# Sixteen 64-byte reads of the weights at the head of ScalarE's DMA queue, in a bilinear kernel

## Chip, core and metric

The kernel runs on one core of one Trainium2 chip. The metric is the device time of one execution in microseconds; where several executions were made, their median is given.

## What is computed

```python
batch, dim_i, dim_j, dim_k = 32, 256, 256, 128
# x [32, 256], y [32, 256], weight [128, 256, 256], all float32
out = np.einsum('bi,bj,kij->bk', x, y, weight)      # [32, 128] float32
```

For each k the 256 x 256 matrix of weights is multiplied from the left by a row of x and from the right by a row of y. The weights are 33.55 MB and are read once.

## The kernel before

**Layout.** The 128 values of k are cut into 32 groups of 4 (`G = 32`, `KK = 4`). A group is a tile of 128 partitions (4 values of k by 32 blocks of i) with 8 x 256 elements each (`IC = 8` rows of i by 256 of j), 1 MB in float32. TensorE multiplies the tile by a block-diagonal copy of x (`xblk`, 128 x 128 in bfloat16 for each of the 8 `ic`), adds the 8 steps up in PSUM, and gets for each k and batch row a row of 256 values of j. VectorE multiplies this by y (`y4`) and sums over j into `acc`, one column per group. At the end `acc` goes to the output in one DMA.

**Loads.** Thirty of the 32 groups are loaded by GpSimd's DMA queue (line 120, eleven transfers, listed in `LOADS`), which casts float32 to bfloat16 on the way into `w_sb`. The sizes fall towards the end: 2, 4, 8, 8, 4, 2 and 1 groups, then the last group in four parts. The other two groups (`FIRST`, 0 and 16) are loaded as float32 by SyncE's queue (line 133) into `w_f`, and ScalarE casts them into `w_sb` (line 177, four instructions). x and y are loaded by ScalarE's queue (lines 128 and 129). Each transfer has a semaphore of its own, waited for at 16.

**Order.** All these DMA instructions are moved by hand to the head of the program (`head[:at_hw] + hw + head[at_hw:at_sw] + sw + head[at_sw:]`), ahead of a start barrier that releases all engines at about 5.5 us. So ScalarE's queue begins with x and y, SyncE's with the two float32 groups, GpSimd's with its eleven loads. Behind the barrier ScalarE does its table load and its casts; VectorE makes `x_rep` (line 191), `xt` (197), `mask` (204), `xblk` (209) and then, from y, `yt` (218), `y_rep` (221) and `y4` (226).

**Compute.** `UNITS` gives the order in which groups are used: 16, 8, 4, 2, 1 and 1 groups. TensorE runs one unit after the other (matmul at line 236), each waiting for the loads that it needs and for free PSUM banks; VectorE follows with a product (293) and a sum (297), or both in one instruction for the two last units (301). Line 310 stores the output, and line 314 clears the semaphores, while SyncE waits for the store.

Of the kernel before, what the change touches and what calls it, by code (L numbers as in the profile page):

```python
# [36 lines left out]
def kernel(  # L37
# [7 lines left out]
    nc = tc.nc  # L45
    P = 128
    f32 = mybir.dt.float32
# [18 lines left out]
    def sbuf(name, shape, dtype):  # L66
        return nc.alloc_sbuf_tensor(name, shape, dtype).ap()

    def rows_of(groups):


        step = G // len(groups)
        assert all(g == groups[0] + n * step for n, g in enumerate(groups))
        v = weight.rearrange("(u s) (ip ic) j -> s ip u (ic j)", s=step, ic=IC)
        return v[groups[0]]

    def w_of(groups):
        at = [place_of[g] for g in groups]
        step = at[1] - at[0] if len(at) > 1 else 1
        assert all(a == at[0] + n * step for n, a in enumerate(at))  # L80
        return w_sb[:, at[0]:at[-1] + 1:step, :]

    w_sb = sbuf("w_sb", [P, G, IC * J], bf16)
    w_f = sbuf("w_f", [P, len(FIRST), IC * J], f32)
    x_sb = sbuf("x_sb", [B, I], f32)
    y_sb = sbuf("y_sb", [B, J], f32)
    ident = sbuf("ident", [P, P], f32)
# [12 lines left out]
    s_w = [nc.alloc_semaphore(f"w{n}") for n in range(len(LOADS))]  # L100
    sem_of = {
        (g, ic): s
        for s, (groups, lo, hi) in zip(s_w, LOADS) for g in groups for ic in range(lo, hi)
    }
    s_f = [nc.alloc_semaphore(f"f{g}") for g in FIRST]
    s_x = nc.alloc_semaphore("x")
    s_y = nc.alloc_semaphore("y")
    s_pool = nc.alloc_semaphore("pool")
    s_act = nc.alloc_semaphore("act")
    s_pe = nc.alloc_semaphore("pe")  # L110
    s_dve = nc.alloc_semaphore("dve")
    s_fin = nc.alloc_semaphore("fin")
    s_out = nc.alloc_semaphore("out")
    sems = [*s_w, *s_f, s_x, s_y, s_pool, s_act, s_pe, s_dve, s_fin]
    nums = [s.num for s in sems]
    assert nums == list(range(nums[0], nums[0] + len(nums)))

# [3 lines left out]
            out=w_of(groups)[:, :, lo * J:hi * J],  # L121
            in_=rows_of(groups)[:, :, lo * J:hi * J],
        ).then_inc(s, 16).ins
        for (groups, lo, hi), s in zip(LOADS, s_w)
    ]

    hw = [
        nc.scalar.dma_start(out=x_sb, in_=x).then_inc(s_x, 16).ins,
        nc.scalar.dma_start(out=y_sb, in_=y).then_inc(s_y, 16).ins,
    ]  # L130
    for n, g in enumerate(FIRST):
        hw.append(
            nc.sync.dma_start(
                out=w_f[:, n:n + 1, :], in_=rows_of((g,)),
# [13 lines left out]
    for blk in blocks:  # L148
# [15 lines left out]
    pool, act, v, pe, sp = nc.gpsimd, nc.scalar, nc.vector, nc.tensor, nc.sync  # L164
# [4 lines left out]
        out=ident, in_=ident, compare_op=mybir.AluOpType.not_equal, fill=1.0,  # L169
        base=0, pattern=[[-1, P]], channel_multiplier=1,  # L170
    )._wait_ge(s_pool, 1).then_inc(s_pool, 1)


    for n, g in enumerate(FIRST):
        for h in range(2):
            lo, hi = h * IC * J // 2, (h + 1) * IC * J // 2
            c = act.copy(out=w_sb[:, place_of[g], lo:hi], in_=w_f[:, n, lo:hi])  # L177
            if h == 0:
                c._wait_ge(s_f[n], 16)
            c.then_inc(s_act, 1)  # L180
# [4 lines left out]
    def done(ins):  # L185
# [6 lines left out]
        out=x_rep,  # L192
        in_=x_sb.rearrange("b (ip ic) -> b ic ip", ic=IC).unsqueeze(3)
        .to_broadcast([B, IC, IP, KK]),
    )._wait_ge(s_x, 16))
    for q in range(Q):
        c = v.transpose(  # L197
            out=xt[q * 32:(q + 1) * 32, :, :],
            in_=x_rep[:, :, q * IP // Q:(q + 1) * IP // Q, :],
# [5 lines left out]
        out=mask, in_=ident.rearrange("p (ip kk) -> p kk ip", kk=KK), axis=AX, op=add,  # L205
    )._wait_ge(s_pool, 2))

    for kk in range(KK):
        c = v.tensor_scalar(  # L209
            out=xblk[:, :, :, kk], in0=xt, scalar1=mask[:, kk:kk + 1],  # L210
# [8 lines left out]
        out=yt, in_=y_sb.rearrange("b (jb j) -> b jb j", j=32),  # L219
    )._wait_ge(s_y, 16))  # L220
    t = done(v.tensor_copy(  # L221
        out=y_rep, in_=yt.unsqueeze(3).to_broadcast([B, J // 32, B, KK]),
    )._wait_ge(s_dve, t))
    BQ = B // Q
    for q in range(Q):
        c = v.transpose(  # L226
            out=y4[q * 32:(q + 1) * 32, :].rearrange("p (jb j) -> p jb j", j=32),
            in_=y_rep[:, :, q * BQ:(q + 1) * BQ, :],
# [22 lines left out]
    for u, unit in enumerate(UNITS):  # L251
# [40 lines left out]
        if n_g > 1:  # L292
            t = done(v.tensor_tensor(  # L293
                out=prod, in0=sums, in1=y4.unsqueeze(1).to_broadcast([P, n_g, J]), op=mult,
# [3 lines left out]
                out=acc[:, unit[0]:unit[-1] + 1:unit[1] - unit[0]], in_=prod, axis=AX, op=add,  # L298
            )._wait_ge(s_dve, t))
        else:  # L300
            done(v.tensor_tensor_reduce(  # L301
                out=prod[:, 0, :], in0=sums[:, 0, :], in1=y4, scale=1.0, scalar=0.0,
# [44 lines left out]
```

## Time and profile before

| | |
|---|---|
| median of 9 runs | 84.71 us (84.62 to 84.98) |
| the profiled execution | 84.66 us, its span 83.4 us (83.36) |
| granted TensorE clock, mean | 0.959 |
| busy in the span | PE 33.8 us, DVE 24.7, ACT 5.3, POOL 8.3 |
| read from HBM | 33.62 MB |

The span runs from the first to the last instruction of the program; the execution's own time has 1.3 us more around it. Times in the profile count from the start of the span. The DMA queues are named by number: q0 is GpSimd's, q1 SyncE's, q10 ScalarE's. All of them run on the same 16 DMA engines of the core. The bytes of a packet are those written: a 4096-byte packet of q0 has read 8192 bytes of float32. The trace keeps the start, size, duration and queue of every packet, not the engine that moved it; a packet of 4 bytes is the write that counts a semaphore up.

### The profile page before, as it was taken

The numbers are of one execution on the slowest core, as the hardware profiler recorded it, in microseconds if no ns is written. First come the engines' busy times: TensorE is split into PE (matmuls) and PEld (weight loads), VectorE is DVE, ScalarE is ACT, GpSimd is POOL, SyncE is SP. The second block draws the span as 40 slices with busy tenths as digits, with TensorE's granted clock in tenths as the row PEclk, the third lists the DMA queues.
The fourth block names the chain that finished last, engine by engine and source line by source line (L and its number), as shares of the span: only waits on it lengthen the run. The fifth ranks groups of instructions, "written<-read, shape, count | busy, mean of one in ns | idle before, by whom it ended". The sixth has DMA issues, their size and how long they took to land.

```text
span 83.4 us, 257 instructions
## 1 busy us (share of the span) xinstructions
PE 33.8 (41%) x136; PEld 4.3 (5%) x43; DVE 24.7 (30%) x28; ACT 5.3 (6%) x5; POOL 8.3 (10%) x17
## 2 busy tenths in 40 slices
PE   0000000000000000000099999999007999999780
PEld 0000000000000000000000000000000000122330
DVE  0038596000000000000000000000999930299992
ACT  0039920000000000000000000000000000000000
POOL 5999300000000000000000000000000000000000
PEclk9999999999999999999999999999965579999999
DMA  3999999999999999999999999999999999999970
GB/s 134 379 383 291 218 210 220 216 212 210 212 218 218 218 210 212 212 218 220 214 210 214 212 218 218 218 210 212 212 218 218 216 210 214 210 220 216 195 112 8
DMA packets 4928, 17.91 MB, mean 215 GB/s; under 512 B 384, under 2 KB 832, under 8 KB 4672
## 3 DMA queue, kind: packets, MB, share of 16 engines
q0 software_dynamic: 4400, 15.73, 94.2%
q1 hardware_dynamic: 432, 2.11, 6.5%
q10 hardware_dynamic: 96, 0.07, 0.3%
HBM read 33.62 MB, written 0.02 MB: 404 GB/s over the span
## 4 chain that ended last, share of the span: by engine, by line
DMA 47%; PE 41%; DVE 6%; POOL 2%; issue 1%; another core or an unknown queue 1%; POOLq 0%
DMA w_sb<-in_weight_dram 47%; PE ps L236 41%; DVE tmp L293 5%; POOL w_sb L120 2%; DVE tmp L301 1%; POOL const-float32-0.0 L331 0%; POOLq L331 0%; POOL const-uint8-127 L331 0%; POOL const-float32-1.0 L331 0%; DVE acc L301 0%
## 5 line engine op out<-in xcount | busy, mean ns | idle before, releaser
L236 PE MATMUL ps<-w_sb,xblk 128*128 128x512 bf16 (+1 forms) x136 | 33.8, 410 | 47.6 <-DMA w_sb<-in_weight_dram 42.9
L293 DVE TENSOR_TENSOR tmp<-ps,y 128x4096 f32<-128x4096 f32 (+3 forms) x4 | 8.6, 2153 | 49.8 <-PE ps L236 49.8
L297 DVE TENSOR_REDUCE acc<-tmp 128x16 f32<-128x4096 f32 (+3 forms) x4 | 8.6, 2154 | 0.1
L236 PEld LDWEIGHTS ps<-w_sb,xblk 128*128 128x128 bf16 x43 | 4.3, 101 | 76.9 <-DMA w_sb<-in_weight_dram 42.7
L120 POOL DMA_DIRECT2D w_sb<-in_weight_dram x11 | 7.5, 699 | 0.6 <-issue 0.6
L177 ACT CAST w_sb<-w_f 128x1024 bf16<-128x1024 f32 x4 | 4.0, 1042 | 0.1
L191 DVE COPY x_rep<-x_sb 32x1024 f32<-32x1024 f32 x1 | 0.7, 736 | 5.6 <-PEq L331 5.6
L226 DVE STREAM_TRANSPOSE y<-y_rep 32x256 f32<-32x256 f32 x4 | 1.7, 434 | 0.1
L197 DVE STREAM_TRANSPOSE xt<-x_rep 32x256 f32<-32x256 f32 x4 | 1.7, 434 | 0.1
L177 ACT ACT_TABLE_LOAD x1 | 1.3, 1283 | 5.6 <-PEq L331 5.6
L209 DVE TENSOR_SCALAR xblk<-xt,mask 128x256 bf16<-128x256 f32 x4 | 1.4, 501 | 0.0
L301 DVE CUSTOM_DVE_ANT_0 tmp<-ps,y 128x256 f32<-128x256 f32 x2 | 0.8, 420 | 0.3 <-PE ps L236 0.3
L221 DVE COPY y_rep<-yt 32x1024 f32<-32x1024 f32 x1 | 0.7, 680 | 0.0
L204 DVE TENSOR_REDUCE mask<-ident 128x4 f32<-128x128 f32 x1 | 0.4, 383 | 1.0 <-POOL ident L168 1.0
L218 DVE STREAM_TRANSPOSE yt<-y_sb 32x256 f32<-32x256 f32 x1 | 0.4, 449 | 0.0
L168 POOL TENSOR_SCALAR_AFFINE_SELECT ident<-ident 128x128 f32<-128x128 f32 x1 | 0.3, 290 | 0.1
L167 POOL MEMSET ident<- 128x128 f32 x1 | 0.3, 279 | 0.0
L301 DVE DVE_READ_ACCUMULATOR2_ANT acc<- 128x1 f32 x2 | 0.2, 84 | 0.0
L331 POOL MEMSET const-float32-0.0<- 128x1 f32 x1 | 0.1, 99 | 0.2 <-issue 0.2
L331 POOL MEMSET const-bfloat16-1.0<- 128x1 bf16 x1 | 0.1, 102 | 0.0
L331 POOL MEMSET const-uint8-127<- 128x1 uint8 x1 | 0.1, 102 | 0.0
L331 POOL MEMSET const-float32-1.0<- 128x1 f32 x1 | 0.1, 99 | 0.0
## 6 DMA issues: line engine op xcount, KB each, us to landing
w_sb<-in_weight_dram POOLq DMA_DIRECT2D x2, 4096.0 KB, 48.5
w_sb<-in_weight_dram POOLq DMA_DIRECT2D x2, 2048.0 KB, 43.6
w_f<-in_weight_dram SPq DMA_DIRECT2D x2, 1024.0 KB, 6.8
w_sb<-in_weight_dram POOLq DMA_DIRECT2D x2, 1024.0 KB, 41.2
w_sb<-in_weight_dram POOLq DMA_DIRECT2D x1, 512.0 KB, 72.6
w_sb<-in_weight_dram POOLq DMA_DIRECT2D x1, 256.0 KB, 73.3
w_sb<-in_weight_dram POOLq DMA_DIRECT2D x1, 128.0 KB, 73.4
w_sb<-in_weight_dram POOLq DMA_DIRECT2D x2, 64.0 KB, 73.1
```

The lines of the kernel that those rows point to most:

```text
L120: nc.gpsimd.dma_start(out=w_of(groups)[:, :, lo * J:hi * J], in_=rows_of(groups)[:, :, lo * J:hi * J],).then_inc(s, 16).ins
L177: c = act.copy(out=w_sb[:, place_of[g], lo:hi], in_=w_f[:, n, lo:hi])
L191: t = done(v.tensor_copy(out=x_rep, in_=x_sb.rearrange("b (ip ic) -> b ic ip", ic=IC).unsqueeze(3) .to_broadcast([B, IC, IP, KK]),)._wait_ ...
L197: c = v.transpose(out=xt[q * 32:(q + 1) * 32, :, :], in_=x_rep[:, :, q * IP // Q:(q + 1) * IP // Q, :],)
L204: t = done(v.tensor_reduce(out=mask, in_=ident.rearrange("p (ip kk) -> p kk ip", kk=KK), axis=AX, op=add,)._wait_ge(s_pool, 2))
L209: c = v.tensor_scalar(out=xblk[:, :, :, kk], in0=xt, scalar1=mask[:, kk:kk + 1], scalar2=None, op0=mult,)
L221: t = done(v.tensor_copy(out=y_rep, in_=yt.unsqueeze(3).to_broadcast([B, J // 32, B, KK]),)._wait_ge(s_dve, t))
L226: c = v.transpose(out=y4[q * 32:(q + 1) * 32, :].rearrange("p (jb j) -> p jb j", j=32), in_=y_rep[:, :, q * BQ:(q + 1) * BQ, :],)
L236: return pe.add_instruction(mybir.InstMatmult(name=nc.get_next_instruction_name(), engine=mybir.EngineType.PE, ins=[pe.lower_ap(rhs), pe.l ...
L293: t = done(v.tensor_tensor(out=prod, in0=sums, in1=y4.unsqueeze(1).to_broadcast([P, n_g, J]), op=mult,)._wait_ge(s_pe, n_pe))
L297: done(v.tensor_reduce(out=acc[:, unit[0]:unit[-1] + 1:unit[1] - unit[0]], in_=prod, axis=AX, op=add,)._wait_ge(s_dve, t))
L301: done(v.tensor_tensor_reduce(out=prod[:, 0, :], in0=sums[:, 0, :], in1=y4, scale=1.0, scalar=0.0, op0=mult, op1=add, accum_out=acc[:, uni ...
```

## The change

ScalarE's queue gets a first transfer, ahead of x and y: 16 rows of 16 float32 values (64 bytes) from the first matrix of the weights, 16 KB apart, one row to each of 16 partitions of a new small tile `touch`. Nothing reads the tile. ScalarE waits for its semaphore ahead of its casts, and the semaphore joins those that are cleared at the end.

```diff
+    touch = sbuf("touch", [16, 16], f32)
...
+    s_touch = nc.alloc_semaphore("touch")
...
-    sems = [*s_w, *s_f, s_x, s_y, s_pool, s_act, s_pe, s_dve, s_fin]
+    sems = [*s_w, *s_f, s_touch, s_x, s_y, s_pool, s_act, s_pe, s_dve, s_fin]
...
     hw = [
+        nc.scalar.dma_start(
+            out=touch, in_=weight[0].rearrange("(e r) j -> e (r j)", e=16)[:, :16],
+        ).then_inc(s_touch, 16).ins,
         nc.scalar.dma_start(out=x_sb, in_=x).then_inc(s_x, 16).ins,
         nc.scalar.dma_start(out=y_sb, in_=y).then_inc(s_y, 16).ins,
     ]
...
+    act.wait_ge(s_touch, 16)
     for n, g in enumerate(FIRST):
```

In the order of the instructions on each engine, ScalarE's queue has one DMA more at its head and its table load one wait more. The order on the other four engines is as before.

## The prediction

> **What bounds the kernel now.** I read the table of queues first, then the chain that ended last, then the waits of TensorE, then the first 5 us in half-microsecond stretches, because the change acts only there.
>
> ```profile
> q0 software_dynamic: 4400, 15.73, 94.2%
> q1 hardware_dynamic: 432, 2.11, 6.5%
> q10 hardware_dynamic: 96, 0.07, 0.3%
> HBM read 33.62 MB, written 0.02 MB: 404 GB/s over the span
> ```
>
> GpSimd's queue (q0) and SyncE's (q1) hold the 16 DMA engines for about the whole span. The weights are 33.55 MB in float32, so nearly all that is read is the weights. In the packet records each engine takes one 8 KB piece every 305 ns (8 groups, 64 pieces per engine, land 19.52 us apart). 256 pieces per engine by 0.305 us is 78.1 us of the 83.4 us. The kernel is its stream of weights, and what is left is when the stream starts, what is put between its packets, and 2.6 us behind its last byte.
>
> ```profile
> 75.88 0.14 another core or an unknown queue
> ...
> 77.95 0.53 another core or an unknown queue
> ...
> 79.55 0.18 another core or an unknown queue
> ```
>
> These lines of the chain of waits, between pieces of TensorE work, are late landings of weights: TensorE has caught up by 75.9 us. If the stream ended earlier by up to 0.5 us, TensorE would follow. The last matmul, the product on VectorE and the output store come behind that and don't change.
>
> ```profile
> 1.00:1.50 0.50, 0.00 (x0) 0.00 (x0) 0.00 (x0) 0.00 (x0) 0.44 (x1) 1.00 0.49 174
> 1.50:2.00 0.50, 0.00 (x0) 0.00 (x0) 0.00 (x0) 0.00 (x0) 0.50 (x2) 1.00 0.71 285
> 2.00:2.50 0.50, 0.00 (x0) 0.00 (x0) 0.00 (x0) 0.00 (x0) 0.50 (x1) 1.00 1.07 442
> ...
> 3.50:4.00 0.50, 0.00 (x0) 0.00 (x0) 0.00 (x0) 0.00 (x0) 0.50 (x2) 1.00 1.09 369
> 4.00:4.50 0.50, 0.00 (x0) 0.00 (x0) 0.00 (x0) 0.00 (x0) 0.50 (x2) 1.00 0.86 324
> 4.50:5.00 0.50, 0.00 (x0) 0.00 (x0) 0.00 (x0) 0.00 (x0) 0.50 (x1) 1.00 1.01 410
> ```
>
> The last column is GB/s. Two dips matter: the stream isn't at full rate before 2.0 us, and it loses some between 3.5 and 4.5 us, which is where y's small packets come through. At full rate (16 engines by 8192 bytes per 305 ns: 430 GB/s) the second dip is 0.5 x (1 - 369/430) + 0.5 x (1 - 324/430) = 0.19 us.
>
> The first dip has a shape. In the packet records x (two packets of 1 KB and a semaphore write on each engine) starts at 1.18 us; on 13 engines its semaphore is written by 1.42 us. The first weight packets start at 1.41 to 1.66 us on twelve engines, about 0.15 us behind that engine's x semaphore. On three engines x's second packet comes at 1.78 to 1.90 us, and four engines start on the weights only at 1.96 to 2.07 us. The table of queues for 1.45 to 3.40 us shows the late ones:
>
> ```profile
> q1 hardware_dynamic: 88, 0.72, 91.7%
> q10 hardware_dynamic: 6, 0.00, 0.5%
> ```
>
> Six packets on ScalarE's queue: three late x packets and three semaphore writes. The lag never heals, for all engines run at one rate. The sixteen landings of the first GpSimd load spread from 11.64 to 12.23 us, those of the fourth load over 0.60 us too, the last ones from 80.26 to 80.77 us. TensorE needs all sixteen. So the end is set by an engine some 0.5 us behind the earliest, and its four followers stand at 0.41, 0.38, 0.35 and 0.33 us.
>
> **What the Trainium skill says.** "DMA: Bandwidth & Descriptors", section "Queues, rings and completion order": each engine goes round its rings and drains a whole packet of one before it turns to the next. The trace agrees for y: its issue is over by 1.01 us, and its first packets run at 3.43 us, late in the first 8-piece weight transfer. The same page, "Why a DMA increments its semaphore by 16 and not by 1": the outer dimension fixes the number of engines, so a transfer of 16 rows has one row on each of 16. The trace of before has no such transfer; x has two rows on each. "Perfetto Trace Analysis", section "DMA Instruction — HWDGE (DVE, Sync)": the descriptor generator is shared and locked while in use. The trace is not against it: x's issue (0.12 to 0.54 us) lies inside the first weight issue (0.00 to 0.63 us), and their packets start one behind the other.
>
> **The change part by part.**
>
> 1. A third issue on ScalarE, ahead of x and y. x's took 417 ns and y's 437 ns, so x's moves from 0.12 to about 0.57 and y's to about 1.02 us; ScalarE is free at 1.46 instead of 1.01 us. Behind it stands only the release of the start barrier, at 5.5 us: hidden by 4 us. Without that cover it would cost 0.44 us.
> 2. ScalarE's wait on the touch. Behind it are the table load (5.55 us) and the four casts. x landed 2.2 us after its issue, so the touch has landed by about 2.5 us and the wait is over when it is reached. Were it 3 us longer, the casts would end at 14 instead of 10.96 us, and their reader TensorE waits for a weight load until 41.88 us. Zero.
> 3. x lands later: with y's 4.5 us from issue to landing, at 0.57 + 4.5 = 5.1 us; VectorE reads it at 5.59 us. y lands by 8.5 us at the latest (the second weight transfer, issued ahead of it, lands then); it is read at 10.80 us. VectorE's preparation ends at 13.83 us and has 28 us to spare. Zero.
> 4. The touch's own bytes: 16 x 64 bytes. x's packet of 1 KB takes 44 ns and a semaphore write 9 ns, so at most some 50 ns per engine, before the weights arrive. SyncE's two issues and GpSimd's eleven keep their order; GpSimd's first packets come at 5.4 us with 2.4 us of q1 in front of them.
> 5. One more semaphore to clear at the end: the clear is one instruction of 139 ns at 82.4 us, beside the output's landing. Zero.
> 6. What stands ahead of the weights on each engine. Before: two packets of x and a semaphore, some 85 ns, and about 0.5 us on the late engines. After: one packet and a semaphore. Earlier by 0.04 us on an ordinary engine, by up to 0.5 us on a late one. From below: nothing, if the touch is late on some engines as x was (no row tells why x was). From above: the slow four drop to the level of the next ones (0.33 us) and that group, the tail of x's spread, shrinks to about 0.2 us: 0.52 - 0.2 = 0.3 us. I take 0.25.
> 7. x's packets now come inside the weight stream, where y's were, and y's come later. Two packets 43 ns apart plus a semaphore are 0.09 us per engine if only their own time counts; 0.19 us if they cost what y's dip did; nothing where they fall on an engine that is ahead. I take 0.05, since before they also cost 0.04 (already counted in 6), and since the semaphore waits of y and of a weight transfer coincide, as they do now.
>
> The sum: -0.25 + 0.05 = -0.20 us on the profiled execution, 84.66 us (83.36 us of span and 1.30 around it), which gives 84.46. The median of nine runs is 84.71, so this execution was slightly quick, perhaps with a slightly smaller lag; against the median the same sum gives **84.51 us**. The runs spread from 84.62 to 84.98, and 0.2% (0.17 us) is about what a measurement of this kernel can tell from no change.
>
> **The rivals.**
>
> *A. The late engines go* (as summed): 84.51, from 84.3 to 84.65. For it: the late x packets, the 0.15 us between x's semaphore and the first weights, a lag that stays to the last byte. Against: why three engines were late is not in the trace. Chance 0.50.
>
> *B. The lag is only moved, or it is chance of the run:* the touch is itself late on some engines, or the four would start late without any small transfer ahead. Then gain and interleaving cancel: 84.71, within 0.12. It includes that the touch does nothing at all: had it been meant to spare the weights a slow first access, the first weight packets of before take 329 to 355 ns against 309 later, so no more than 0.05 us is there. Chance 0.27.
>
> *C. Slower.* In the stream of SyncE's first transfer x's packets cost what y's did, 0.19 us, y's then cost it again among the second transfer's and GpSimd's packets, and the start gains nothing. One dip more: 84.71 + 0.19 = 84.90; with a late touch in front of the weights, up to 85.0. It decides as soon as the slowest engine starts on the weights less than 0.19 us sooner than before. Chance 0.23.
>
> **How the numbers follow.** Faster by over 0.2% (below 84.54): 0.38 of A's 0.50, 0.03 of B: 0.41. Within: 0.12 + 0.21 + 0.02 = 0.35. Slower: 0.03 + 0.21 = 0.24. A alone gives 84.3 to 84.65; holding the time 8 times in 10 needs B and most of C: **84.27 to 84.95**.
>
> **What would show it.** In the changed trace: 64-byte packets near 1.2 us, one per engine; no ScalarE packets between 1.45 and 3.4 us; weights at 1.4 to 1.65 us on all engines, so more than 285 GB/s in 1.5 to 2.0 us; x's packets near 3.4 us; last landings within 0.35 us of each other. For B the spread stays at 0.5 us; for C the stretches to 8 us show a second dip. A move of over 0.5 us either way, or a new wait at 5.6 or 10.8 us, would make the whole account wrong.

## The result, and the profile after

The changed kernel is slower: 85.24 us in the median of 16 runs (84.88 to 85.64), against 84.88 us for the kernel before in 53 runs (84.58 to 85.10). The ratio is 1.0045, with a 95% interval of 1.0033 to 1.0056, so 0.28 to 0.48 us. The forecast was 84.51 us, with an upper end of 84.95. Part of the distance is the base: the nine runs shown before had a median of 84.71 us, and the larger sample lies 0.17 us higher.

The profiled execution after took 85.29 us (span 84.0 us), so it is a usual one. The one before, of 84.66 us, was among the quick ones of its kernel. The queue table after, with packets, MB and share of the 16 engines:

```profile
q0 software_dynamic: 4400, 15.73, 93.5%
q1 hardware_dynamic: 432, 2.11, 6.9%
q10 hardware_dynamic: 128, 0.07, 0.3%
HBM read 33.62 MB, written 0.02 MB: 400 GB/s over the span
```

ScalarE's queue has 32 packets more (16 of data, 16 of semaphore), the rest is unchanged; the same bytes go at 400 instead of 404 GB/s. The chain of waits after still has the late weights between the pieces of TensorE work:

```profile
76.22 0.43 another core or an unknown queue
...
78.58 0.48 another core or an unknown queue
...
80.14 0.18 another core or an unknown queue
```

TensorE has caught up by 76.2 us as before (75.9), and waits longer for the next load: 0.43 instead of 0.14 us. So the loss is in the weight stream, not in the compute. The first microseconds after, by stretch (the last three columns are granted clock, DMA share and GB/s):

```profile
1.00:1.50 0.50, 0.00 (x0) 0.00 (x0) 0.00 (x0) 0.00 (x0) 0.44 (x1) 1.00 0.70 150
1.50:2.00 0.50, 0.00 (x0) 0.00 (x0) 0.00 (x0) 0.00 (x0) 0.50 (x2) 1.00 0.55 131
2.00:2.50 0.50, 0.00 (x0) 0.00 (x0) 0.00 (x0) 0.00 (x0) 0.50 (x1) 1.00 1.22 442
...
3.50:4.00 0.50, 0.00 (x0) 0.00 (x0) 0.00 (x0) 0.00 (x0) 0.50 (x2) 1.00 0.95 344
4.00:4.50 0.50, 0.00 (x0) 0.00 (x0) 0.00 (x0) 0.00 (x0) 0.50 (x2) 1.00 1.19 408
4.50:5.00 0.50, 0.00 (x0) 0.00 (x0) 0.00 (x0) 0.00 (x0) 0.50 (x1) 1.00 0.80 313
```

From 1.5 to 2.0 us the engines move 131 GB/s, where the quick execution of before had 285. In the packet records all 16 engines start on the weights between 1.41 and 1.67 us, as foreseen, but every first weight packet takes 0.51 to 0.64 us instead of about 0.33. The last number in each of these lines is the time from issue to landing in us; before:

```profile
x_sb<-in_x_dram ACTq DMA_DIRECT2D x1, 32.0 KB, 2.2
y_sb<-in_y_dram ACTq DMA_DIRECT2D x1, 32.0 KB, 4.5
```

and after:

```profile
x_sb<-in_x_dram ACTq DMA_DIRECT2D x1, 32.0 KB, 4.7
y_sb<-in_y_dram ACTq DMA_DIRECT2D x1, 32.0 KB, 6.6
touch<-in_weight_dram ACTq DMA_DIRECT2D x1, 1.0 KB, 1.6
```

x has moved from 2.2 to 4.7 us and y from 4.5 to 6.6 us. x now comes where y was, and y where there was no small transfer. The table of queues for 5.0 to 6.5 us has no packet of q10 before,

```profile
q1 hardware_dynamic: 53, 0.43, 69.8%
q0 software_dynamic: 24, 0.10, 33.2%
```

and 43 of them after:

```profile
q1 hardware_dynamic: 52, 0.43, 69.8%
q0 software_dynamic: 20, 0.08, 28.2%
q10 hardware_dynamic: 43, 0.03, 8.3%
```

The last sixteen landings of weights come from 80.58 to 81.38 us (80.26 to 80.77 in the first profile of before), and the mean one at 80.87 instead of 80.46 us.

A first theory came from these records. **Theory 1:** the loss is a slow first weight packet, because only 64 bytes are ahead of it on each engine, and one more small transfer inside the weight stream. **Theory 2:** the touch reads the rows that the first weight packets read, and collides with them. The experiments leave of both only the transfer inside the stream.

### The profile page after: what moved, and what is told of

Same layout as the page of the kernel before. It is cut to its first block, busy times and chain, and to the rows that moved or that the text cites. A ratio compares the mean times of both kernels' runs of the same rounds, so it can differ in the third digit from the quotient of the medians.

```text
span 84.0 us, 259 instructions
## 1 busy us (share of the span) xinstructions
PE 33.6 (40%) x136; PEld 4.3 (5%) x43; DVE 24.7 (29%) x28; ACT 5.3 (6%) x5; POOL 8.3 (10%) x17
## 4 chain that ended last, share of the span: by engine, by line
DMA 47%; PE 40%; DVE 6%; POOL 2%; issue 1%; another core or an unknown queue 1%; POOLq 0%
DMA w_sb<-in_weight_dram 47%; PE ps L244 40%; DVE tmp L301 5%; POOL w_sb L122 2%; DVE tmp L309 1%; POOL const-float32-0.0 L339 0%; POOLq L339 0%; POOL const-uint8-127 L339 0%; POOL const-float32-1.0 L339 0%; DVE acc L309 0%
```

## The experiments

All keep the kernel's code but for the edits shown. The ratio is to the kernel before, run beside them; that kernel against itself gave 1.0004 (0.9992 to 1.0015, e8). The times in the second and third column are rough, in us from the start of the span. e1, e4, e9 and e13 rest on five to seven runs, the others on 13 to 22. A touch of 64 bytes means 64 on each engine.

| kernel | ahead of the weights | small transfers inside the stream, at | median us | ratio (95%) |
|---|---|---|---|---|
| before | x | y at 3.5 | 84.88 | 1 |
| e11, y left out | x | none | 84.88 | 0.9993 (0.9983 to 1.0003) |
| e6 | x | y at 9 to 11 | 84.78 | 0.9989 (0.9980 to 0.9999) |
| e14 | x | y in GpSimd's ring, at 21.5 | 84.81 | 0.9993 (0.9982 to 1.0004) |
| e2 | nothing | x, y at 9 to 11 | 84.93 | 1.0011 (0.9999 to 1.0023) |
| e12, y left out | touch | x at 4 | 85.00 | 1.0009 (0.9999 to 1.0019) |
| e3 | touch | x, y at 9 to 11 | 84.98 | 1.0024 (1.0012 to 1.0036) |
| e15 | touch | x at 3.5, y at 9 to 11 | 85.04 | 1.0026 (1.0015 to 1.0036) |
| e5 | x | y at 3.5, touch at 5 | 85.03 | 1.0025 (1.0011 to 1.0040) |
| **after** | touch | x at 3.5, y at 5 | 85.24 | 1.0045 (1.0033 to 1.0056) |
| e1 | touch, of x | x at 3.5, y at 5 | 85.26 | 1.0053 (1.0035 to 1.0072) |
| e4 | 32 KB of weights | x at 3.5, y at 5 | 85.25 | 1.0052 (1.0033 to 1.0070) |
| e9 | x | y at 3.5, 32 KB at 5 | 85.31 | 1.0059 (1.0043 to 1.0074) |
| e13 | touch | x at 3.5, y at 5, 32 KB at 7 | 85.28 | 1.0039 (1.0022 to 1.0057) |

**What the touch reads, and what is ahead of the weights.**

```diff
# e1: the touch reads x
-            out=touch, in_=weight[0].rearrange("(e r) j -> e (r j)", e=16)[:, :16],
+            out=touch, in_=x[0:16, 0:16],
# e4: two rows of 1 KB on each engine, as x has
-    touch = sbuf("touch", [16, 16], f32)
+    touch = sbuf("touch", [32, 256], f32)
...
-            out=touch, in_=weight[0].rearrange("(e r) j -> e (r j)", e=16)[:, :16],
+            out=touch, in_=weight[0].rearrange("(e r) j -> e (r j)", e=32)[:, :256],
# e2 (from before) and e3 (from after): x and y issued behind the start barrier
-        nc.scalar.dma_start(out=x_sb, in_=x).then_inc(s_x, 16).ins,
-        nc.scalar.dma_start(out=y_sb, in_=y).then_inc(s_y, 16).ins,
...
+    act.dma_start(out=x_sb, in_=x).then_inc(s_x, 16)
+    act.dma_start(out=y_sb, in_=y).then_inc(s_y, 16)
     for n, g in enumerate(FIRST):
```

> The touch as in the changed kernel (16 x 64 bytes, head of ScalarE's queue), but read from x instead of the weights. Theory 1 (what matters is that little stands ahead of the first weight packet on each engine, and that x and y both fall into the weight stream): nothing changes against the changed kernel; about 85.2 us, first weight packets of about 0.6 us, mean landing of SyncE's first transfer near 4.62 us. Theory 2 (the touch reads the same rows as the first weight packets and collides with them): first packets back to 0.33 us, about 0.28 us of the 0.36 us of loss gone, 84.9 to 85.0 us.

> No touch, and x and y issued by ScalarE behind the start barrier, so nothing stands ahead of the weights. Theory 1: the first weight packets take about 0.6 us (nothing has warmed the engines), SyncE's first transfer lands 0.1 to 0.2 us earlier than in the changed kernel, since no small transfer falls into it, and x and y cost their 0.17 us each later among GpSimd's packets; about 84.9 to 85.1 us. Theory 2: first packets of 0.33 us, since nothing collides, and about 84.6 us.

> The touch at the head as in the changed kernel, x and y issued by ScalarE behind the start barrier. It separates the slow first packets (kept) from x and y in SyncE's transfers (gone). Theory 1: first packets still about 0.6 us; the same time as the kernel with an empty head within 0.1 us (84.9 to 85.1). Theory 2: first packets 0.6 us, and 0.28 us slower than the kernel with an empty head. If the touch did warm something, it is faster than the empty head.

> The first transfer has x's shape: 32 rows of 1 KB from the weights, two packets on each engine, in place of 16 x 64 bytes; x and y follow as in the changed kernel. Theory 1: what is ahead of the weights is as in the kernel before, so first weight packets take 0.33 us again, and what remains is one more small transfer in the stream, 0.17 us: 85.0 to 85.1 us. Theory 2: it reads the same rows as the first weight packets too, so they stay at 0.6 us and the time at 85.2 us or more.

e1 is as slow as the changed kernel, and its first packets stay at 0.58 us: theory 2 falls. e4 has first packets of 0.32 us and is just as slow, so the slow first packet isn't needed for the loss. e4 alone doesn't rule it out, for its weights start later, at 1.75 us in the mean against 1.51; the second and third profile of the kernel before, shown next, do: they have slow first packets too (0.61 and 0.45 us in the mean) without its loss. With nothing ahead (e2) the first packets take 0.52 us. In these three profiles and the first one of after, the earliest second weight packets begin between 1.93 and 2.0 us. With nothing ahead the weights also start between 1.41 and 1.68 us, as they do behind x or behind the touch: x and the touch don't hold them up there. Touch alone (e3) against nothing (e2) shows no gain; the ratios, 1.0024 and 1.0011, have overlapping intervals.

**Was the first profile usual?**

> The kernel before, unchanged, for a second profile: the first one was an execution of 84.66 us, quicker than its median of 84.82 to 84.88. Theory of chance: the lag of some engines differs from execution to execution, so the start of the weights, the spread of the landings or their mean differ from the first profile; ratio 1.000, within 0.001. If the first profile is typical: first weight packets from 1.41 to 2.07 us and a mean landing of 4.44 us again.

> The kernel before, for one more profile. If the slow first weight packets and the even start of the second profile are the usual form, they appear again: first packets of 0.5 to 0.68 us, all starts from 1.40 to 1.70 us, last landing near 81.0 us. If the first profile's form is usual: 0.33 us and 80.8 us.

> The changed kernel, for a second profile. If the loss is a mean delay of the stream plus a larger lag of the slowest engine, both appear again: mean last landing 0.15 to 0.2 us behind that of before, slowest engine 0.45 us or more behind the mean. If the lag of the first profile was chance, only the mean delay does.

The kernel before took 84.92 us in its second profile and 84.67 us in its third; the changed kernel took 84.77 us in its second, less than any of its 16 runs above. The first stretches of e8, the kernel before, 84.92 us:

```profile
1.00:1.50 0.50, 0.00 (x0) 0.00 (x0) 0.00 (x0) 0.00 (x0) 0.44 (x1) 1.00 0.99 230
1.50:2.00 0.50, 0.00 (x0) 0.00 (x0) 0.00 (x0) 0.00 (x0) 0.50 (x2) 1.00 0.44 98
```

and of e17, the changed kernel, 84.77 us:

```profile
1.00:1.50 0.50, 0.00 (x0) 0.00 (x0) 0.00 (x0) 0.00 (x0) 0.44 (x1) 1.00 0.42 150
1.50:2.00 0.50, 0.00 (x0) 0.00 (x0) 0.00 (x0) 0.00 (x0) 0.50 (x2) 1.00 0.79 262
```

Here the kernel before has slow first packets (0.54 to 0.68 us, 98 GB/s in 1.5 to 2.0 us), and in the changed kernel eight of the sixteen take no more than 0.37 us (262 GB/s). So the start changes from execution to execution in both kernels. The late x packets and the four late engines of the first profile are in neither of the other two profiles of before, where all weights start by 1.68 us. They aren't unique, though: e11, also with x at the head, has x packets up to 1.98 us and weights that start only at 2.03. Yet the late starts leave the slowest engine no further behind the mean at the end: 0.32 us in the first profile of before, 0.36 and 0.26 in the two without them. e17's slowest engine was 0.23 us behind the mean, against 0.51 in the first profile after: that lag too was in part chance of the execution, as its expectation allowed.

**How much a small transfer costs, and where.** e5 and e9 leave x at the head; a third transfer follows y.

```diff
# e5 (from after): the touch behind x and y;  e9: the same with 32 rows of 1 KB, as in e4
-        nc.scalar.dma_start(
-            out=touch, in_=weight[0].rearrange("(e r) j -> e (r j)", e=16)[:, :16],
-        ).then_inc(s_touch, 16).ins,
         nc.scalar.dma_start(out=x_sb, in_=x).then_inc(s_x, 16).ins,
         nc.scalar.dma_start(out=y_sb, in_=y).then_inc(s_y, 16).ins,
+        nc.scalar.dma_start(
+            out=touch, in_=weight[0].rearrange("(e r) j -> e (r j)", e=16)[:, :16],
+        ).then_inc(s_touch, 16).ins,
# e6 (from before) and e15 (from after): y behind the start barrier
-        nc.scalar.dma_start(out=y_sb, in_=y).then_inc(s_y, 16).ins,
...
+    act.dma_start(out=y_sb, in_=y).then_inc(s_y, 16)
     for n, g in enumerate(FIRST):
# e11, e18 (from before) and e12 (from after): no load of y
-        nc.scalar.dma_start(out=y_sb, in_=y).then_inc(s_y, 16).ins,
...
-        out=yt, in_=y_sb.rearrange("b (jb j) -> b jb j", j=32),
-    )._wait_ge(s_y, 16))
+        out=yt, in_=x_sb.rearrange("b (jb j) -> b jb j", j=32),
+    )._wait_ge(s_x, 16))
# e13 (from after): a fourth transfer, with a tile, a semaphore and a wait like the touch's
...
         nc.scalar.dma_start(out=y_sb, in_=y).then_inc(s_y, 16).ins,
+        nc.scalar.dma_start(
+            out=third, in_=weight[0].rearrange("(e r) j -> e (r j)", e=32)[:, :256],
+        ).then_inc(s_third, 16).ins,
...
# e14 (from before): y third in GpSimd's queue, and gone from ScalarE's
+    sw.insert(2, nc.gpsimd.dma_start(out=y_sb, in_=y).then_inc(s_y, 16).ins)
...
-        nc.scalar.dma_start(out=y_sb, in_=y).then_inc(s_y, 16).ins,
```

> The touch (16 x 64 bytes of the weights) as the third transfer of ScalarE's queue, behind x and y. x is again ahead of the weights. Theory: the loss has two parts, (a) a first weight packet that is slow where only the touch is ahead of it, 0.1 to 0.18 us, and (b) one more small transfer inside the weight stream, about 0.15 us. Here (a) is gone: first weight packets of 0.33 us and SyncE's first landing at 4.44 us in the mean. If (b) is paid per transfer (its semaphore and the turn of the ring): 85.0 us, ratio 1.002. If it is paid by bytes: 84.87, ratio 1.000. Rival (the order of x is what matters, x being late does harm later): 84.87 too; a rival by which the touch itself harms wherever it stands: 85.2.

> As the kernel before with a third transfer of x's shape (32 rows of 1 KB, read from the weights) behind x and y on ScalarE's queue: one small transfer more inside the stream, nothing changed ahead of it. Theory: 0.15 us more, 85.03 us, ratio 1.0018; SyncE's first landing at 4.44 us as before, the first GpSimd landing 0.15 us later than before. If a small transfer inside the stream is free, 84.87.

> x at the head as before, y issued by ScalarE behind the start barrier, so that it falls among GpSimd's packets at 9 to 11 us instead of in SyncE's first transfer. Theory: a small transfer costs about the same 0.15 us wherever it falls in the stream, so SyncE's first landing comes about 0.2 us earlier (4.2 to 4.3 us in the mean), the first GpSimd landing gives it back, and the time is that of before within 0.1%: 84.8 to 84.9. If y in SyncE's transfer is dearer than among GpSimd's packets, it is faster, down to 84.7.

> The kernel before without y's load: VectorE takes x in y's place, so y is left out of the product. x is ahead of the weights, no small transfer falls into the weight stream. Theory (the cost goes by the number of small transfers inside the stream of SyncE's two transfers, about 0.36 us for each by the end of the kernel): one fewer than before, so 84.5 us, ratio 0.996 (0.995 to 0.998). If y's transfer costs only its own bytes, 0.09 us: ratio 0.999.

> The kernel before without y's load (x in y's place), for a second profile. If the slow start of its first profile (x's own packets of up to 0.74 us, weights from 1.4 to 1.8 us) was chance, this one starts as before does and its mean landing is 0.1 to 0.15 us ahead of before's. If it returns, taking y away changes the start.

> The changed kernel without y's load (x in y's place, as in the other kernel of this pair). The touch is ahead of the weights, x alone inside them: one small transfer inside the stream, as in the kernel before. Theory: the time of before, ratio 1.000 (0.9985 to 1.0015), and 0.36 us more than the kernel with x alone at the head. Rival (the touch itself slows the start, by what is ahead of the weights or by reading their rows): slower than before, ratio 1.002 or more.

> The changed kernel with a further transfer of x's shape (32 rows of 1 KB of the weights) behind y: the touch ahead, three small transfers inside the stream. Theory: another 0.36 us on top of the changed kernel, 85.6 us, ratio 1.009 (1.007 to 1.011). If the second one was dear only because x moved out of the free place at the start, or because x lands late, a third costs its 0.09 us: ratio 1.006.

> x at the head as before, y as the third transfer of GpSimd's queue, behind its first two loads: then y stands in the same ring as the weights, with no other ring to turn to. Theory: y costs its own bytes there, 0.1 us, instead of what it costs between two rings; faster than before by 0.1 to 0.25 us, 84.6 to 84.75, ratio 0.997 to 0.999. If a small transfer costs the same in any ring: as y issued behind the barrier, 84.78. If GpSimd's extra issue (0.7 us) delays its later loads: slower than before.

> The changed kernel with y issued behind the start barrier: touch ahead, x inside SyncE's first transfer, y among GpSimd's packets at 9 to 11 us instead of at 5.0 to 6.5 us. If the loss is by place (a small transfer between 5 and 6.5 us, when three rings are active, sets some engines back): most of it is gone, ratio 1.001 to 1.002, 85.0 us. If it is by the number of transfers inside the stream: as the changed kernel, ratio 1.004 or more.

The packet records give a common measure. The bytes of each weight packet are laid over its duration; what a stretch lacks of the full 430 GB/s is lost stream time, in us of the average engine:

| profile | 0 to 3.5 us | 3.5 to 4.5 | 4.5 to 6.5 | 8.5 to 12 | mean last landing | slowest engine behind it |
|---|---|---|---|---|---|---|
| before, three profiles | 1.78, 1.90, 1.84 | 0.22, 0.20, 0.21 | 0.09, 0.15, 0.14 | 0.01, 0.02, 0.01 | 80.46, 80.67, 80.54 | 0.32, 0.36, 0.26 |
| after, two | 1.93, 1.78 | 0.21, 0.21 | **0.27, 0.22** | 0.02, 0.02 | 80.87, 80.58 | 0.51, 0.23 |
| e1 | 1.89 | 0.18 | **0.21** | 0.03 | 80.72 | 0.55 |
| e4 | 1.87 | 0.23 | **0.29** | 0.02 | 80.83 | 0.35 |
| e9 | 1.89 | 0.15 | **0.35** | 0.01 | 80.80 | 0.46 |
| e5 (64 bytes) | 1.88 | 0.21 | 0.14 | 0.03 | 80.63 | 0.21 |
| e15 | 1.90 | 0.17 | 0.09 | **0.14** | 80.67 | 0.37 |
| e2 (x and y) | 1.85 | 0.09 | 0.08 | **0.27** | 80.67 | 0.45 |
| y left out: e11, e18 | 2.09, 1.91 | 0.12, 0.05 | 0.08, 0.14 | 0.01, 0.02 | 80.67, 80.44 | 0.40, 0.26 |

In the mean, a transfer of 32 KB costs 0.11 to 0.15 us of stream in each of these stretches. From 3.5 to 4.5 us the profiles that have one there lose about 0.20 us, and the kernels with none there 0.05 to 0.12. From 4.5 to 6.5 us it is 0.27 in the mean of the six profiles with a third transfer of 32 KB (the five shown and e13). The twelve without it lose 0.13 in the mean, but from 0.08 to 0.20 singly, so one profile alone couldn't show it. From 8.5 to 12 us it is 0.14 for one (e15) and 0.27 for two (e2), against 0.02. By an estimate from the durations of its packets, 0.09 us of this are the packets themselves, as prediction step 7 had them.

In the changed kernel the transfer that is added inside the stream is y, pushed from 3.5 to 5.0 us, with x in its old place. Nothing is given back at the start: the first column differs as much between two executions of a kernel as between kernels. Over all profiles, those not in the table among them, it is 1.91 us in the mean of nine with x at the head and 1.94 in the mean of seven with the touch there.

What the average engine loses isn't all. In the five profiles with a third transfer of 32 KB on ScalarE's queue (both of after, e1, e4, e9) the slowest engine ends 0.42 us behind the mean, in the three of before 0.31. The last landing is 81.18 us against 80.87 in these: 0.31 us, of which 0.21 is the mean engine and the rest the lag. Singly the lags overlap (e2, with no third transfer, has 0.45). The spread of the sixteen landings of GpSimd's fourth load, at 61 us, tells the two groups better apart: 0.77 to 0.95 us in five of the six profiles with such a transfer (0.51 in e17), 0.43 to 0.75 in the other twelve.

e15 differs from the changed kernel only in when y is issued, behind the barrier instead of at the head, and has 1.0026 against 1.0045. It still pays 0.12 us for y in the average engine. So part of the loss belongs either to the place, 5.0 to 6.5 us, or to a third issue at the head of ScalarE's queue as such; no run has one without the other. e5 speaks for the second, at least in part: its third transfer is only the 64-byte touch, for which its profile shows no more than 0.02 us, and its median is still slower by 0.09 to 0.34 us.

Some expectations missed. e5 came out at 1.0025, as a cost per transfer would have it, but its profile was one of the quick executions (84.79 us, of 84.74 to 85.50), so it doesn't show where the median's 0.2 us go. e12, with the touch ahead and one transfer inside, has the time of before within the range set for it (1.0009), which speaks against a large cost of the touch at the start. e11 was to gain 0.36 us by having one transfer fewer, and gained 0.07%, with an interval that reaches from a gain of 0.17% to a loss of 0.03%; its first profile had a start 0.25 us worse than before's mean, its second (84.64 us) a start 0.07 us worse. e13 was to lose another 0.36 us, and has the time of the changed kernel, although its profile has the fourth transfer's dip (0.12 us lost from 6.5 to 8.5 us, against 0.06 after). So the cost by the median is not 0.36 us for each transfer: only ScalarE's third is that dear. For the second and the fourth the intervals leave room for the 0.11 to 0.15 us of the packet records as well as for nothing.

e14, y in GpSimd's own ring, gains no more than e6. Its y runs at 21.5 us, where the stream loses 0.08 us more than in before (20 to 24 us), and VectorE waits 11.0 us for it, which TensorE's first weights at 42 us hide. e6, y behind the barrier, has the lowest median of the versions that compute the whole product: 84.78 us, ratio 0.9989 with an interval that just leaves 1 out. It is faster than the changed kernel; among so many comparisons, that it is also faster than the kernel before isn't sure.

## Why the prediction was wrong

**What held.** The kernel is its weight stream, and the end moves with the slowest engine's last landing. The third issue on ScalarE, its wait, the late x and y, the extra semaphore (steps 1 to 3 and 5) show no new wait that reaches the end: VectorE takes up x at 5.59 us as before, and ScalarE's table load begins at 5.61 instead of 5.55. ScalarE's casts did have to wait 1.5 us for the second of SyncE's transfers,

```profile
ACT w_sb L185 <- DMA w_f<-in_weight_dram: 1.5, 1, 1.5
```

and ended near 12.5 us, far ahead of TensorE's first use at 42.5 us. Step 4 priced the touch at no more than 50 ns at the head; no run shows more there that is clear of the scatter. From 1.45 to 3.40 us ScalarE's queue (q10) has no packet,

```profile
q1 hardware_dynamic: 79, 0.65, 94.9%
```

and the weights start by 1.67 us on all engines, as the last part foresaw. The other two signs named there failed: 131 GB/s (262 in e17) from 1.5 to 2.0 us where more than 285 were to be seen, and last landings 0.80 us apart (0.38 in e17) where it said within 0.35.

**Step 6 failed**, and with it the sign. It took the four late engines of one profile as the kernel's own and booked 0.25 us for their removal. Two further profiles of the same kernel have no late engine, and their slowest engine still ends 0.36 and 0.26 us behind the mean, against 0.32 in the first. The profile with the late engines even has the smallest loss of the three at the start (1.78 us), since its first packets were quick. There was nothing to gain: the starts lose 1.78 to 1.93 us in both kernels. Nor does x ahead of the weights set their start on an ordinary engine. With nothing there (e2) they begin at the same 1.41 to 1.68 us, so the 0.15 us between x's semaphore and the first weights was no sign that the weights wait for x, and the 0.04 us for an ordinary engine had no ground.

**Step 7 was mis-sized**: 0.05 us net for x inside the stream, where the profiles show 0.15 us in the mean for the transfer that is now at 5 us, against 0.09 for its own packets. The 0.04 us that was set against it, which step 6 had counted already, isn't there, and no run shows a saving by coinciding semaphore waits. A larger lag of the slowest engine, 0.1 us on these few profiles, was not in the sum at all.

**Rival C was the right one**: one dip more, nothing gained at the start. Its price, 0.19 us, is about what the average engine loses; the 0.36 us measured is nearly twice that, and the lag accounts for some 0.1 us of the rest. It was given 0.23, and its time was built on a base 0.17 us too low.

**What stays open.** Whether the loss beyond the 0.15 us comes with the place at 5.0 to 6.5 us or with a third issue at the head of ScalarE's queue, whatever its size (e5): a run with a third issue whose packets fall elsewhere is missing. How some engines are set further back: the records don't name the engine, so the slow ones can't be followed through that stretch. Why e13 has no larger median than the changed kernel. And what makes the first weight packet 0.33 or 0.6 us long: it isn't what the touch reads (e1), and it differs between executions of the same program.

## What to carry to other kernels

When a kernel is one stream of DMA at full rate, every further transfer, however small, either fits ahead of the stream or is paid inside it: a transfer of 64 bytes per engine at the head of a queue had no cost of its own that could be told from the scatter, but it pushed two 32 KB loads one place back, and a second one came to lie inside the stream, for 0.15 us of the average engine and 0.36 us in the median. Keep the place ahead of the stream for transfers that must be made anyway, and try issuing the others late: y at 9 us was cheaper here than at 5 (e15). And don't read a start-up lag of half a microsecond from one execution: see whether it comes back in a second profile, and whether it moves the end there, before booking a gain on it.

## What the runs showed of the hardware that was not expected

The first 8 KB packet of an engine took 0.32 to 0.36 us on the engines that started early in the first profile of the kernel before, 0.54 to 0.68 in the second and 0.39 to 0.49 in the third, against 0.31 us later in the stream; with 2 KB of weights ahead on each engine (e4) it took 0.31 to 0.37 us but started 0.24 us later, so the second packets began at 1.98 us or later all the same. From 12 us on no profile of a kernel without a small transfer there loses more than 0.1 us of stream up to 75 us, and a spread of the engines that is there at 12 us stays: the sixteen landings lay 0.95 us apart at 12 and at 61 us in the changed kernel, and 0.72 us apart at both times in e8.
